# Index score products that may break into projection chains at once, with rope tables, row scales and weight rooms rearranged, in one layer of a hybrid streaming encoder

## The chip, the cores and the metric

The kernel runs on one core of one Trainium2 chip. A core has five engines that work side by side: TensorE (PE) for matrix products, VectorE (DVE), ScalarE (ACT), GpSimd (POOL) and SyncE (SP), which issues the DMAs. The metric is the device time of one execution in microseconds. The kernel before takes 1736.39 us (median of 3 runs, 1735.83 to 1738.16).

## The reference

One layer is run for two request groups that share weights: a prompt of 1024 new positions, and 32 sample positions with 512 cached ones. Width is 1024, heads have 64 channels, there are 8 heads in each mixer.

```python
h = rmsnorm(x);  z = h @ w_in        # q/k/v of mixer A, indexer q, k, weights, q/k/v of mixer B, gates
q_a, k_a = rope(rmsnorm(q_a, g_qn)), rope(rmsnorm(k_a, g_kn));  q_i, k_i = rope(q_i), rope(k_i)
# mixer A: the indexer scores all keys, and each query attends to its top k of them
score = einsum('bqhl,bqh->bql', relu(q_i @ k_i), w_i);  idx = top_k(score, topk)
o_a = softmax(q_a @ k_a[idx]) @ v_a[idx]
# mixer B: stick-breaking attention, strictly causal
o_b = (exp(log_sigmoid(s) - tail(softplus(s)))) @ v_b
h = x + (sigmoid(gate_a) * (o_a @ w_ba) + sigmoid(gate_b) * (o_b @ w_bb)) @ w_out
y = h + relu(rmsnorm(h) @ w_up)**2 @ w_down
```

The outputs are y and the new keys and values of both mixers and of the indexer, for both groups. Everything is float32.

## The kernel before, in words

**Numbers.** Each float32 matrix product is done as three products of a faster format: an operand is split into a high part (a ScalarE copy that rounds) and a low part (the rest, by a subtraction on GpSimd or VectorE), and high x high, high x low and low x high are added. The 1056 positions form nine tiles: eight of 128 rows and one of 32 (`NEW`). A weight unit is 128 x 512: one DMA into `wst`, the high half `wh` from ScalarE, the low half `wl` from GpSimd. `wh` and `wl` have a ring of five rooms each (`WB`).

**The order of the work.** Nothing is issued when it is written in the code. A planner (`Plan`) records every operation with its engine, rank and an estimated cost. When a pool of memory is closed, it plays the five engines forward and issues, on each, the ready operation of the lowest rank and then of the oldest number. The order so found is fixed at build time, and each engine follows it strictly. Ranks are `FAST` 0, `PREP` 1 (weight loads and splits), `MAIN` 2, `FILL` 3 (the long projection chains) and `SLOW` 4. A rule concerns TensorE alone: while it is in a `FILL` chain, another ready product may break in only when it has been ready for longer than its patience:

```python
if eng == PE and self.row is not None and n.row is None and at - n.ready < n.wait:
```

Patience is `WAIT[0]` = 1000 ns for the whole first part, up to the end of mixer A's projection.

**The stages in turn.** (1) The index stage: x is scaled and split, the indexer's queries are projected in two halves (`index_projection`, tiles `s` in three PSUM banks), rotated, and transposed (`rr`); the sums of squares give the row scales `rs` (128 x 9). (2) `spread_rs` makes from `rs` a row `rb` of 1056 scales that is the same on all partitions: nine times `ones` times one column of `rs` (tile `rsb`, on GpSimd), a TensorE transpose into a `t` bank, a ScalarE copy. Every projection's result is multiplied by `rb` on VectorE, and only then is its `pj` bank (two of them) free. `index_keys` scales the indexer's keys `kr`, also on GpSimd. (3) `project_b` for four head pairs: chains of 24 products per part for q, k and v of mixer B (`FILL`), and, recorded between pairs 1 and 2, `index_scores`: 12 score parts times 8 heads, each of two products into an `s` bank (`kih`, `kil`), a relu on ScalarE in place, and a multiply-add on VectorE into `score`. (4) `top_k_begin`: 31 rounds of a binary search, in two groups of tiles, each round counting scores on ScalarE and VectorE (`junk`, `cand`, `small`), at rank `SLOW`. (5) `rope_tables` loads the cosines and sines into the projection pool and multiplies them by the gains of q and k on VectorE (`tabc`, `tabs`). `project_a` for four head pairs: per tile a row block of 24 products, then VectorE multiplies by the tables (`ta`, `tb`), GpSimd adds, ScalarE squares; at the end transposes `qk` into `az`. Each pair needs four weight units plus two for v. (6) `top_k` makes the masks; three gates; then the pools are closed, and attention opens its own in the same room. (7) Attention of the first 512 positions of mixer B and then A, with gate chains as filling; `load_o` reads the outputs back from DRAM and splits them, four tiles (e = 4 to 7, ring `sg` of three rooms) before the branch products of mixer B can end; then branch, output projection and the feed-forward part, with the attention of the second half beside it.

The functions of the diff, with the lines of the profile:

Of the kernel before, what the change touches and what calls it, by code (L numbers as in the profile page):

```python
# [9 lines left out]
F32 = mybir.dt.float32  # L10
F32R = mybir.dt.float32r
BF16 = mybir.dt.bfloat16
I32 = mybir.dt.int32
AF = mybir.ActivationFunctionType
ALU = mybir.AluOpType
# [5 lines left out]
KB = D // 128  # L21
# [3 lines left out]
T = SEQ + DEC  # L25
NT = 9
H = 8
HD = 64
# [12 lines left out]
NEW = 8  # L41
WB = 5
# [3 lines left out]
GATES = (2, 3, 4)  # L46
SUMS = 3
ORDER = (*range(8, 16), 5, 6, 7)
WAIT = (1000, 0, 1500)
TOPK = (("a", [2, 3, 4, 7], (2, 7), 0), ("b", [5, 6, 8], (5, 6), 16))  # L50
EARLY, PACE = 14, 3
LATER = 3
FAST, PREP, MAIN, FILL, SLOW = 0, 1, 2, 3, 4
# [365 lines left out]
class Layer:  # L419
# [18 lines left out]
        self.nc.scalar.copy(h, x)  # L438
        self.nc.gpsimd.tensor_sub(l, x, h.bitcast(F32))

    def unit(self, src):

        nc = self.nc
        key = (src.tensor.name, src.offset)
        if key in self.begun:
            return self.begun.pop(key)
        with nc.rank(PREP):
            st = nc.tile(self.wpool, [128, 512], F32, "wst", bufs=3)
            h = nc.tile(self.wpool, [128, 512], F32R, "wh", bufs=WB)
            l = nc.tile(self.wpool, [128, 512], F32R, "wl", bufs=WB)  # L450
            nc.sync.dma_start(st, src)
            self.split(h, l, st)
        return h, l
# [79 lines left out]
    def run(self):  # L533
        nc, a = self.nc, self.a
# [8 lines left out]
        c = lambda shape, dt, name: nc.tile(self.const, shape, dt, name)  # L543
# [41 lines left out]
        self.index_setup()  # L585
        nc.patience = WAIT[0]
        for sl in ((0,), (1, 2), (3,), (4, 5), (6, 7, 8)):
# [3 lines left out]
            for s in sl:  # L591
                self.index_projection(0, s)
                if s >= LATER:
                    self.row_square(s - LATER)
        self.constants()
        for s in range(NT):
            self.index_projection(1, s)
            if s < LATER:
                self.row_square(NT - LATER + s)
# [9 lines left out]
        mk = nc.open("mask", "right")  # L609
        self.mask = [nc.tile(mk, [128, 128 * (t + 1)], BF16, f"mask{t}") for t in range(8)]  # L610
        self.mask.append(nc.tile(mk, [128, LS], BF16, "mask8"))
        self.top = nc.open("top", "right")
        self.index_scores()
        for p in range(2, 4):
            self.project_b(p)
        with nc.rank(SLOW):
# [3 lines left out]
        self.early(*(a["w_qka"][0, j] for j in range(4)))  # L620
        nc.close(self.pr, self.ik)
        self.pr = nc.open("proja")
        self.rope_tables()
        self.sample(self.pr)
        for p in range(4):
            self.project_a(p)
# [2 lines left out]
        for e in GATES:  # L629
            self.gate(e)  # L630
        self.early(*(a["w_g"][e, j] for e in (8, 9) for j in range(2)))
        nc.close(self.pr, self.top)
        nc.patience = WAIT[1]


# [123 lines left out]
    def spread_rs(self):  # L759

        nc = self.nc
        for sl in GROUPS:
            pt = self.bank("t")
            n = sum(rows(s) for s in sl)
            for i, s in enumerate(sl):
                b = nc.tile(self.ip, [128, 128], F32, "rsb", bufs=2)
                nc.gpsimd.tensor_scalar(b, self.ones, self.rs[:, s:s + 1], None, op0=ALU.mult)
                m = rows(s)
                nc.tensor.transpose(pt[:, i * 128:i * 128 + m], b[:m], self.ident[:m, :m])
            nc.scalar.copy(self.rb[:, 128 * sl[0]:128 * sl[0] + n], pt[:, :n])  # L770


    def index_setup(self):
# [173 lines left out]

    def top_k(self):

        nc, tp, tx, size = self.nc, self.top, self.top, self.size  # L950
        for g in self.groups:
            tf = nc.tile(tp, [128, g.n], I32, "tf" + g.name)
            nc.vector.tensor_scalar(tf, g.thr, 0, None, op0=ALU.bitwise_xor)
            tf = tf.bitcast(F32)
            if g.act:
                low = nc.tile(tp, [128, g.n], F32, "low" + g.name)
                for j, t in enumerate(g.tiles):
                    m, L, k = size(t)
                    if t not in g.act:
                        nc.vector.tensor_copy(low[:m, j:j + 1], tf[:m, j:j + 1])  # L960
                        continue
                    pen = nc.tile(tx, [128, 1024], F32, "pen", tag="pre", bufs=1)
                    nc.vector.tensor_scalar(
                        pen[:m, :L], self.score[t][:m], tf[:m, j:j + 1], BIG, op0=ALU.is_lt, op1=ALU.mult)
                    nc.vector.tensor_tensor_reduce(
                        out=pen[:m, :L], in0=pen[:m, :L], in1=self.score[t][:m], scale=1.0, scalar=BIG,
                        op0=ALU.add, op1=ALU.min, accum_out=low[:m, j:j + 1])
                tf = low
            above = g.count(tf, ALU.is_gt)
            need = nc.tile(tp, [128, g.n], F32, "need" + g.name)  # L970
            for j, t in enumerate(g.tiles):
                m, L, k = size(t)
                nc.vector.tensor_scalar(
                    need[:m, j:j + 1], above[:m, j:j + 1], -1.0, float(k), op0=ALU.mult, op1=ALU.add)
                sc = self.score[t][:m]
                eq = nc.tile(tx, [128, 1024], BF16, "eq", tag="junkv", bufs=1)
                pre = nc.tile(tx, [128, 1024], F32, "pre", bufs=1)
                nc.vector.tensor_scalar(eq[:m, :L], sc, tf[:m, j:j + 1], None, op0=ALU.is_equal)
                nc.vector.tensor_tensor_scan(pre[:m, :L], eq[:m, :L], eq[:m, :L], 0.0, op0=ALU.add, op1=ALU.bypass)
                nc.vector.scalar_tensor_tensor(  # L980
                    pre[:m, :L], pre[:m, :L], need[:m, j:j + 1], eq[:m, :L], op0=ALU.is_le, op1=ALU.mult)
                nc.vector.scalar_tensor_tensor(
                    pre[:m, :L], sc, tf[:m, j:j + 1], pre[:m, :L], op0=ALU.is_gt, op1=ALU.add)
                nc.gpsimd.tensor_scalar(self.mask[t][:m, :L], pre[:m, :L], -NEG, NEG, op0=ALU.mult, op1=ALU.add)
        for j in range(4):
            if j:
                nc.sync.dma_start(self.mask[8][32 * j:32 * j + 32], self.mask[8][0:32])
            nc.sync.dma_start(self.fqs[32 * j:32 * j + 32], self.fq[:DEC, NEW, j::4])


    def rope_tables(self):
        nc, a, pr = self.nc, self.a, self.pr
        self.tc_ = nc.tile(pr, [128, NT, 2, HD], F32, "tabc")
        self.ts_ = nc.tile(pr, [128, NT, 2, HD], F32, "tabs")
        C = nc.tile(pr, [128, NT, HD], F32, "ropec")
        S = nc.tile(pr, [128, NT, HD], F32, "ropes")
        g = nc.tile(pr, [128, 2, HD], F32, "gqk")
        nc.sync.dma_start(C, a["rope_c"])
        nc.sync.dma_start(S, a["rope_s"])
        nc.sync.dma_start(g, a["g_qk"].unsqueeze(0).to_broadcast([128, 2, HD]))  # L1000
        for j in range(2):
            nc.vector.tensor_mul(self.tc_[:, :, j], C, g[:, j].unsqueeze(1).to_broadcast([128, NT, HD]))
            gx = g[:, j].rearrange("p (s e) -> p s e", s=2)[:, ::-1, :].unsqueeze(1).to_broadcast([128, NT, 2, 32])
            nc.vector.tensor_mul(
                self.ts_[:, :, j].rearrange("p t (s e) -> p t s e", s=2),
                S.rearrange("p t (s e) -> p t s e", s=2), gx)

    def project_v(self, p, mixer, w, vout):

# [48 lines left out]

    def project_a(self, p):
        nc, pr, a = self.nc, self.pr, self.a  # L1060
        units = [self.unit(a["w_qka"][p, j]) for j in range(4)]
        qk = nc.tile(pr, [128, NT, 4, HD], F32, "qk", bufs=1)
        ss = nc.tile(pr, [128, NT, 4], F32, "ss", bufs=2)
        nc.gpsimd.memset(qk[:, NEW], 0.0)
# [25 lines left out]
        rsb = self.rs.unsqueeze(2).to_broadcast([128, NT, 4])  # L1090
# [15 lines left out]
        for j, dst in ((0, self.dq), (1, self.dk)):  # L1106
            for sl in GROUPS:
                n = sum(rows(s) for s in sl)
                pt = self.bank("t")
# [234 lines left out]
    def load_o(self, g, j, tag="sg", bufs=3):  # L1344

        nc = self.nc
        for e in range(4 * j, 4 * j + 4):
            if not g.i and e == H // 2 - 1:
                for i, o in enumerate(self.kept):
                    z = slice(64 * i, 64 * i + 64)  # L1350
                    with nc.rank(FAST):
                        nc.scalar.copy(g.h[z, e], o)
                        nc.vector.tensor_sub(g.l[z, e], o, g.h.bitcast(F32)[z, e])
                continue
            with nc.rank(PREP):
                o32 = nc.tile(self.op, [128, g.w], F32, "o32", tag=tag, bufs=bufs)
                nc.sync.dma_start(o32, self.do[2 * e:2 * e + 2, :, g.lo:g.lo + g.w].rearrange("g e t -> (g e) t"))
                self.split(g.h[:, e], g.l[:, e], o32)

# [300 lines left out]
    def ffn_group(self, g, late=iter(())):  # L1660
# [62 lines left out]
        def beside(n):  # L1723
# [3 lines left out]
            while done >= PACE:  # L1727
                done -= PACE
                nc.patience = WAIT[2]
                with nc.behind():  # L1730
                    next(late, None)
                nc.patience = WAIT[1]

# [100 lines left out]
```

## Time and profile before

| | |
|---|---|
| median of 3 runs | 1736.39 us (1735.83 to 1738.16) |
| profiled execution, its own time | 1734.1 us |
| span of its instructions | 1732.3 us |
| PE busy | 1707.9 us (99%) |
| DVE, ACT, POOL busy | 1225.2, 1046.0, 1006.3 us |
| mean granted TensorE clock | 0.999 |

The span runs from the first instruction to the last. An engine is busy while an instruction of its runs, not while it waits. Products overlap in the array, so the time that a product takes up is read from start to start and not from its duration. Every operation is recorded by one helper, so all rows bear its line, L410, and are told apart by the tiles: `rsb<-ones,rs` writes `rsb` and reads `ones` and `rs`. "SPq" is SyncE's queue of DMA issues. In the list of waits a row gives the engine that waited, the tile, who released it, the total, the number and the longest.

### The profile page before, as it was taken

How to read it: one execution, taken by the hardware profiler on the slowest of the kernel's cores; microseconds unless marked ns; L12 is line 12 of the kernel's file. 1: busy time of each engine (PE TensorE's matmuls, PEld its weight loads, DVE VectorE, ACT ScalarE, POOL GpSimd, SP SyncE). 2: the span in 40 equal slices, each digit the busy share in tenths (PEclk: the TensorE clock that was granted, in tenths of full speed). 3: DMA queues.
4: the chain of work that ended last, by engine and by line, in shares of the span. 5: the costliest groups of instructions: out<-in, count | busy, mean ns of one | idle time of the engine just before them, and what ended most of it. 6: DMA issues, size and time to landing. Idle time of an engine off the chain costs nothing.

```text
span 1732.3 us, 32764 instructions
## 1 busy us (share of the span) xinstructions
PE 1707.9 (99%) x11154; PEld 1569.7 (91%) x11154; DVE 1225.2 (71%) x2474; ACT 1046.0 (60%) x2274; POOL 1006.3 (58%) x838
## 2 busy tenths in 40 slices
PE   8999999999999999999999999999999999999999
PEld 7889998999999889988888888888889999999999
DVE  8545578999966645899987777675455674766667
ACT  6544488887245666777765665462524685747473
POOL 5533231334465676799974544586467794646563
PEclk9999999999999999999999999999999999999999
DMA  6344352444665767656277475574675656556565
GB/s 216 117 140 125 106 148 98 137 138 138 181 176 152 189 200 208 191 166 186 88 220 223 142 246 172 183 240 169 237 254 184 181 169 193 170 178 176 177 179 175
DMA packets 190424, 301.78 MB, mean 174 GB/s; under 512 B 31281, under 2 KB 60561, under 8 KB 190257
## 3 DMA queue, kind: packets, MB, share of 16 engines
q1 hardware_dynamic: 189824, 299.35, 56.7%
q8 instruction: 88, 1.44, 0.3%
q14 instruction: 80, 0.65, 0.1%
q10 hardware_dynamic: 432, 0.34, 0.1%
HBM read 211.80 MB, written 87.70 MB: 173 GB/s over the span
## 4 chain that ended last, share of the span: by engine, by line
PE 86%; DVE 5%; DMA 4%; POOL 2%; issue 2%; ACT 2%; SPq 0%; ACTq 0%; DVEq 0%; POOLq 0%
PE pj L410 62%; PE s L410 13%; PE t L410 4%; PE o L410 4%; PE pd L410 3%; DMA o<-do 1%; DVE rem L410 1%; POOL wl L410 1%; DMA k<-dk 1%; DVE xl L410 1%; DVE tt L410 1%; DMA wst<-w_up 0%; DVE junk L410 0%; ACT wh L410 0%; ACT xh L410 0%
## 5 line engine op out<-in xcount | busy, mean ns | idle before, releaser
L410 PE MATMUL pj<-xh,wh 128*128 128x512 f32 (+1 forms) x1808 | 618.6, 343 | 2.4 <-ACT xh L410 1.8
L410 PE MATMUL pj<-xh,wl 128*128 128x272 f32 (+1 forms) x1808 | 617.5, 342 | 0.6 <-POOL wl L410 0.6
L410 PE MATMUL pj<-xl,wh 128*128 128x512 f32 (+1 forms) x1808 | 616.4, 342 | 0.0
L410 POOL TENSOR_TENSOR wl<-wst,wh 128x512 fp32r<-128x512 f32 x243 | 346.1, 1431 | 248.2 <-ACT wh L410 218.2
L410 PEld LDWEIGHTS pj<-xh,wh 128*128 128x128 f32 x1808 | 340.5, 189 | 35.5 <-ACT xh L410 1.9
L410 PEld LDWEIGHTS pj<-xh,wl 128*128 128x128 f32 x1808 | 340.4, 188 | 33.6 <-POOL wl L410 1.3
L410 PEld LDWEIGHTS pj<-xl,wh 128*128 128x128 f32 x1808 | 340.6, 188 | 32.5 <-issue 0.2
L410 ACT CAST wh<-wst 128x512 fp32r<-128x512 f32 x260 | 159.9, 621 | 139.6 <-PE pj L410 93.9
L410 POOL TENSOR_TENSOR wl<-raw,wh 128x512 fp32r<-128x512 f32 x84 | 119.7, 1429 | 98.2 <-ACT wh L410 93.9
L410 DVE TENSOR_TENSOR_SCAN rem<-rem 128x896 f32<-128x896 f32 (+6 forms) x66 | 124.2, 1899 | 22.7 <-ACT rem L410 19.3
L410 ACT CAST wh<-raw 128x512 fp32r<-128x512 f32 x118 | 73.3, 623 | 83.4 <-PE pj L410 50.6
L410 ACT ACTIVATE junk<-score,cand 128x384 bf16<-128x384 f32 (+1 forms) x124 | 115.9, 935 | 8.0 <-DVE cand L410 5.9
L410 POOL TENSOR_TENSOR p<-p,rem 128x895 f32<-128x895 f32 (+6 forms) x66 | 110.3, 1684 | 17.7 <-DVE rem L410 16.7
L410 DVE TENSOR_TENSOR tt<-t,tt 128x512 fp32r<-128x512 f32 (+2 forms) x168 | 100.1, 619 | 27.1 <-ACT tt L410 26.3
L410 ACT CAST tt<-t 128x512 fp32r<-128x512 f32 (+2 forms) x168 | 85.9, 539 | 45.9 <-PE t L410 30.9
L410 PEld LDWEIGHTS o<-tt,v 128*128 128x128 f32 x640 | 93.2, 189 | 12.9 <-DVE tt L410 3.2
L410 PE MATMUL o<-tt,v 128*128 128x256 f32 (+1 forms) x640 | 100.5, 278 | 1.5 <-DVE tt L410 1.1
L410 PE MATMUL pj<-gh,wl 128*128 128x272 f32 x352 | 101.3, 289 | 0.0
L410 PE MATMUL pj<-gl,wh 128*128 128x272 f32 x352 | 101.1, 288 | 0.0
L410 PE MATMUL pj<-gh,wh 128*128 128x272 f32 x352 | 101.1, 289 | 0.0
L410 POOL TENSOR_TENSOR wl<-rb,wh 128x512 fp32r<-128x512 f32 x55 | 77.3, 1406 | 34.3 <-ACT wh L410 30.1
L410 PE MATMUL s<-k,q 128*128 128x384 f32 (+5 forms) x384 | 94.8, 357 | 2.0 <-DMA k<-dk 1.0
(337 smaller groups left out, 4002.6 us busy)
## 6 DMA issues: line engine op xcount, KB each, us to landing
q<-dq SPq DMA_DIRECT2D x64, 256.0 KB, 5.3
k<-dk SPq DMA_DIRECT2D x48, 256.0 KB, 3.8
v<-dv SPq DMA_DIRECT2D x48, 256.0 KB, 4.0
raw<-w_down SPq DMA_DIRECT2D x47, 256.0 KB, 3.4
wst<-w_up SPq DMA_DIRECT2D x43, 256.0 KB, 3.0
wst<-w_g SPq DMA_DIRECT2D x42, 256.0 KB, 3.9
raw<-w_up SPq DMA_DIRECT2D x42, 256.0 KB, 3.1
wst<-w_down SPq DMA_DIRECT2D x39, 256.0 KB, 3.3
```

The source lines that it names most:

```text
L410: fn(*args, **kw)
```

## The change

1. `WAIT` gets a fourth value, 0, which is the patience of the index score products.
2. `spread_rs`: the nine scalings go from GpSimd to ScalarE (odd tiles) and VectorE (even tiles), all at rank `FAST`, as do the copies into `rb`. Eight of them have one wide tile `rsb` in place of two rooms in turn.
3. The first weight unit of `project_b` is begun before the second half of the index projection.
4. `rope_tables` is recorded before the index scores and has a pool of its own. The cosines and sines are loaded straight into both halves of the tables (four loads in place of two, in runs of 64 elements), and six GpSimd products at rank `SLOW` multiply them by the gains in place.
5. The weights of mixer A's pairs 1 and 3 get four rooms each for `wh` and `wl` in the projection pool; pairs 0 and 2 stay in the common ring.
6. `top_k`'s scratch tiles `pre` and `pen` move to a pool of their own.
7. `load_o`: for the first half, the tile e = 7 is loaded into the ring `pb` in place of `sg`.

```diff
-WAIT = (1000, 0, 1500)
+WAIT = (1000, 0, 1500, 0)
...
-    def unit(self, src):
+    def unit(self, src, room=None):
...
+        pool, n = (room, 4) if room else (self.wpool, WB)
         with nc.rank(PREP):
             st = nc.tile(self.wpool, [128, 512], F32, "wst", bufs=3)
-            h = nc.tile(self.wpool, [128, 512], F32R, "wh", bufs=WB)
-            l = nc.tile(self.wpool, [128, 512], F32R, "wl", bufs=WB)
+            h = nc.tile(pool, [128, 512], F32R, "wh", bufs=n)
+            l = nc.tile(pool, [128, 512], F32R, "wl", bufs=n)
...
         self.constants()
+        self.early(a["w_qb"][0, 0])
...
+        rope = nc.open("rope", "right")
+        self.rope_tables(rope)
         self.top = nc.open("top", "right")
+        nc.patience = WAIT[3]
         self.index_scores()
+        nc.patience = WAIT[0]
...
         self.pr = nc.open("proja")
-        self.rope_tables()
+        self.pre = nc.open("pre", "right")
...
+        rsb = nc.tile(self.pr, [128, T], F32, "rsb", tag="vt", bufs=1)
...
-                b = nc.tile(self.ip, [128, 128], F32, "rsb", bufs=2)
-                nc.gpsimd.tensor_scalar(b, self.ones, self.rs[:, s:s + 1], None, op0=ALU.mult)
+                b = rsb[:, 128 * s:128 * s + 128] if s != NEW else nc.tile(self.ip, [128, 128], F32, "rsb", bufs=1)
+                with nc.rank(FAST):
+                    if s % 2:
+                        nc.scalar.activation(b, self.ones, AF.Copy, scale=self.rs[:, s:s + 1])
+                    else:
+                        nc.vector.tensor_scalar(b, self.ones, self.rs[:, s:s + 1], None, op0=ALU.mult)
...
-            nc.scalar.copy(self.rb[:, 128 * sl[0]:128 * sl[0] + n], pt[:, :n])
+            with nc.rank(FAST):
+                nc.scalar.copy(self.rb[:, 128 * sl[0]:128 * sl[0] + n], pt[:, :n])
...
-        C = nc.tile(pr, [128, NT, HD], F32, "ropec")
-        S = nc.tile(pr, [128, NT, HD], F32, "ropes")
...
+        for tab, src in ((self.tc_, a["rope_c"]), (self.ts_, a["rope_s"])):
+            for j in range(2):
+                nc.sync.dma_start(tab[:, :, j], src)
         for j in range(2):
...
+            with nc.rank(SLOW):
+                c = self.tc_[:, :, j]
+                nc.gpsimd.tensor_mul(c, c, g[:, j].unsqueeze(1).to_broadcast([128, NT, HD]))
+                for i in range(2):
+                    z = self.ts_[:, :, j, 32 * i:32 * i + 32]
+                    nc.gpsimd.tensor_mul(z, z, g[:, j, 32 - 32 * i:64 - 32 * i].unsqueeze(1).to_broadcast([128, NT, 32]))
...
-        units = [self.unit(a["w_qka"][p, j]) for j in range(4)]
+        units = [self.unit(a["w_qka"][p, j], pr if p % 2 else None) for j in range(4)]
...
-                o32 = nc.tile(self.op, [128, g.w], F32, "o32", tag=tag, bufs=bufs)
+                if not g.i and e == KB - 1:
+                    o32 = g.tmp("o32", "pb", 3)
+                else:
+                    o32 = nc.tile(self.op, [128, g.w], F32, "o32", tag=tag, bufs=bufs)
```

More of the change, by code (lines that the diff above doesn't have):

```diff
@@ L631, in run @@
         self.early(*(a["w_g"][e, j] for e in (8, 9) for j in range(2)))
-        nc.close(self.pr, self.top)
+        nc.close(self.pr, self.pre, self.top, rope)
         nc.patience = WAIT[1]
@@ L948, in top_k @@
     def top_k(self):
-        nc, tp, tx, size = self.nc, self.top, self.top, self.size
+        nc, tp, tx, size = self.nc, self.top, self.pre, self.size
         for g in self.groups:
@@ L975, in top_k @@
                 sc = self.score[t][:m]
-                eq = nc.tile(tx, [128, 1024], BF16, "eq", tag="junkv", bufs=1)
+                eq = nc.tile(tp, [128, 1024], BF16, "eq", tag="junkv", bufs=1)
                 pre = nc.tile(tx, [128, 1024], F32, "pre", bufs=1)
@@ L988, in top_k, with rope_tables @@
             nc.sync.dma_start(self.fqs[32 * j:32 * j + 32], self.fq[:DEC, NEW, j::4])
[L991 to L994, printed above, removed]
-        C = nc.tile(pr, [128, NT, HD], F32, "ropec")
-        S = nc.tile(pr, [128, NT, HD], F32, "ropes")
-        g = nc.tile(pr, [128, 2, HD], F32, "gqk")
-        nc.sync.dma_start(C, a["rope_c"])
-        nc.sync.dma_start(S, a["rope_s"])
+    def rope_tables(self, pool):
+        nc, a = self.nc, self.a
+        self.tc_ = nc.tile(pool, [128, NT, 2, HD], F32, "tabc")
+        self.ts_ = nc.tile(pool, [128, NT, 2, HD], F32, "tabs")
+        g = nc.tile(pool, [128, 2, HD], F32, "gqk")
         nc.sync.dma_start(g, a["g_qk"].unsqueeze(0).to_broadcast([128, 2, HD]))
+        for tab, src in ((self.tc_, a["rope_c"]), (self.ts_, a["rope_s"])):
+            for j in range(2):
+                nc.sync.dma_start(tab[:, :, j], src)
         for j in range(2):
[L1002 to L1006, printed above, removed]
+            with nc.rank(SLOW):
[4 more added lines that the diff above has]
+                    nc.gpsimd.tensor_mul(z, z, g[:, j, 32 - 32 * i:64 - 32 * i].unsqueeze(1).to_broadcast([128, NT, 32]))
     def project_v(self, p, mixer, w, vout):
```

## The prediction

> **What bounds the kernel now.** I read first the engines' busy time, then the list of who TensorE (PE) waited for, then the busy time by stretch.
>
> ```profile
> PE 1707.9 (99%) x11154; PEld 1569.7 (91%) x11154; DVE 1225.2 (71%) x2474; ACT 1046.0 (60%) x2274; POOL 1006.3 (58%) x838
> ```
> ```profile
> PE s L410 <- ACT ih L410: 5.2, 1, 5.2
> PE t L410 <- POOL rsb L410: 2.4, 5, 0.8
> PE s L410 <- DVE small L410: 2.1, 1, 2.1
> PE pj L410 <- ACT xh L410: 1.8, 1, 1.8
> PE t L410 <- DVE az L410: 1.4, 1, 1.4
> ...
> PE pj L410 <- POOL wl L410: 0.6, 2, 0.3
> ```
> ```profile
> 280.00:360.00 80.00, 76.27 (x590) 73.11 (x589) 74.82 (x258) 71.08 (x157) 28.86 (x36) 1.00 0.41 121
> 440.00:480.00 40.00, 40.00 (x254) 36.13 (x253) 36.83 (x59) 8.61 (x19) 14.91 (x11) 1.00 0.55 168
> ```
>
> PE sets the end: it is idle 1732.3 - 1707.9 = 24.4 us in all, and the change takes no product away. So only what PE loses in idle time, or at a lowered clock, can be won. Four waits that the edits touch stand in the list: 2.4 (the row scales), 2.1 (the first row blocks of mixer A), 1.8 (attention outputs), 1.4 (az). The 5.2 at the very start is not touched. In the stretches (columns: length, PE, weight load, VectorE, ScalarE, GpSimd) PE is idle 3.73 us from 280 to 360, where VectorE (DVE) is busy 74.82 of 80; from 440 to 480 it isn't idle at all. All five engines run an order written at build time, each strictly in turn; a wait therefore holds everything behind it.
>
> **Row scales (spread_rs).** Here PE loses more than the 2.4 us. The products in order of time, then two stretches' clock:
>
> ```profile
> 81.14 0.28 PE L410 MATMUL pj<-xh,wl 128*128 128x272 f32 x1
> ...
> 85.17 0.33 PE L410 MATMUL t<-ident,rsb 128*128 128x128 f32 x1 [0.25 <-POOL rsb L410]
> 85.25 0.37 PE L410 MATMUL pj<-xh,wh 128*128 128x272 f32 x1
> 85.46 0.29 PE L410 MATMUL pj<-xl,wh 128*128 128x272 f32 x1
> 85.58 0.29 PE L410 MATMUL pj<-xh,wl 128*128 128x272 f32 x1
> ```
> ```profile
> 86.00:89.00 3.00, 3.00 (x14) 2.60 (x13) 0.44 (x1) 1.07 (x2) 1.51 (x2) 0.50 0.04 11
> ```
>
> From 81.14 to 85.25 are 4.11 us. In them one product (0.12, the step from 85.46 to 85.58) and the five transposes of the list of waits (0.08 each, 85.17 to 85.25) do work: 0.52. Lost: 3.6. Then the granted clock is 0.50 for 3.0 us, which loses 3.0 x 0.50 = 1.5. Together 5.1 us. The cause is GpSimd (POOL), which does nine scalings of 0.59 among weight splits:
>
> ```profile
> L410 POOL TENSOR_SCALAR rsb<-ones,rs x9: 592/593/597, 76.2 to 85.7; 128x128 f32<-128x128 f32 x9
> ```
> ```profile
> 70.48 0.16 DVE L410 TENSOR_TENSOR rs<-rs,rw 128x9 f32<-128x9 f32 x1
> ```
> ```profile
> 89.11 0.42 ACT L410 CAST zz<-zb 128x272 fp32r<-128x272 f32 x1
> ```
> ```profile
> L410 DVE TENSOR_SCALAR eq<-score,lowa x4: 420/858/1580, 422.5 to 446.2; 128x384 bf16<-128x384 f32 x1, 128x512 bf16<-128x512 f32 x1, 128x640 bf16<-128x640 f32 x1, 128x1024 bf16<-128x1024 f32 x1
> ```
>
> The scales `rs` are ready at 70.64 (70.48 + 0.16). Afterwards ScalarE (ACT) does four of the scalings, VectorE five, at first rank. No row shows such a 128x128 scaling on either. For ACT I bound it by 0.16 (a tiny instruction) and 0.42 (128x272), and take 0.3, nearer the upper one: 4 x 0.3 = 1.2. For VectorE I bound it by 0.16 and by the slowest one-tensor instruction above, 1.58, and take 0.3 again, somewhat under the 0.42 of 128x384: 5 x 0.3 = 1.5, at worst 5 x 1.58 = 7.9. So the first group (two on each engine) is done at 71.3 to 73.8. The part of `rb` that the first multiplication needs then comes after four transposes (4 x 0.08) and one copy of 512 columns, which I estimate at under 1 us from the 0.42 for 272; with the hand-overs I allow 2 us, and PE needs it only when the two chains in hand end at 81.3. Cover remains in every case: I take 5.0 of it as gained, with 2.5 as the lower bound (the transposes may still stand where PE waits a little) and 5.1 as the upper. GpSimd loses 9 x 0.59 = 5.3 us of work, which lets its weight splits come sooner.
>
> The row for `eq` has 1.58 for 640 columns while its fastest is 0.42 for 384, so some of these wait for something. [...]
>
> **Early weights.** `early(w_qb[0,0])` makes the first unit's low half ready before the first chain. Gain at most the 0.6 us that PE waited for wl in two places; I take 0.3. One more 256 KB load goes ahead of the four of the indexer's second half, beside nothing that PE waits for.
>
> **Index products at patience 0.** Now such a product breaks into a chain only after it has waited 1 us.
>
> ```profile
> L410 PE MATMUL s<-kih,qi x96: 282/339/477, 100.6 to 223.7; 128*128 128x384 f32 x24, 128*128 128x512 f32 x24, 128*128 128x320 f32 x16, 128*32 128x272 f32 x16
> ```
> ```profile
> 154.44 0.29 PE L410 MATMUL s<-kil,qi 128*32 128x272 f32 x1
> 154.57 0.40 PE L410 MATMUL pj<-xl,wh 128*128 128x512 f32 x1
> 154.62 1.35 DVE L410 SCALAR_TENSOR_TENSOR score<-s,wi,score 32x272 f32<-32x272 f32 x3 [1.72 <-ACT s L410]
> 157.31 0.31 PE L410 MATMUL s<-kih,qi 128*128 128x320 f32 x1
> ```
> ```profile
> 150.00:175.00 25.00, 25.00 (x153) 22.57 (x153) 14.34 (x30) 10.71 (x27) 6.35 (x7) 1.00 0.47 151
> 250.00:275.00 25.00, 25.00 (x162) 22.92 (x161) 20.29 (x69) 23.08 (x51) 5.19 (x4) 1.00 0.36 120
> ```
>
> 96 score chunks come in threes, one for each bank: 123.1 / 32 = 3.85 us a round. VectorE has read the last bank at 154.62 + 1.35 = 155.97, the next product starts at 157.31: 1.3 us of waiting. So the scores end up to 32 x 1.3 = 43 us sooner, I take 25. To PE this is worth nothing by itself, since PE is full (25.00 of 25.00) both while scores and while the counts of the top-k that follow run beside the chains. Breaking a chain more often costs nothing that a row shows: from the last index product to the chain's next are 0.13 us, the pace of 272 columns. At 0.01 us of resolution and some 64 more breaks, two changes each, the upper bound is 1.3 us; I take 0.
>
> **Rope tables.** Before, their loads wait for the room of the projection pool, and four VectorE products stand ahead of the first reads of the banks.
>
> ```profile
> 291.64 0.74 DVE L410 TENSOR_TENSOR tabc<-ropec,gqk 128x576 f32<-128x576 f32 x1
> ...
> 294.31 0.41 DVE L410 TENSOR_TENSOR ta<-s,tabc 128x256 f32<-128x256 f32 x1
> ```
> ```profile
> 292.85 0.29 PE L410 MATMUL pj<-xh,wl 128*128 128x272 f32 x1
> 295.20 0.36 PE L410 MATMUL s<-wh,xh 128*128 128x256 f32 x1 [2.06 <-DVE small L410]
> ```
>
> PE starts nothing for 2.35 us, less the one product 2.2. The products go to GpSimd, at last rank, beside the index stage, where it is busy 6.35 of 25. Two are of 576 columns, four of 288; by the 1.43 us of a 512-column GpSimd subtraction (below) that is 2 x 1.6 + 4 x 0.8 = 6.4 us, in 18.65 idle ones. Five loads (four tables, the gains) go through SP's queue there instead of three at 283. If a product stood ahead of a weight split and its load were late, the split would be late; the cover is a whole chain. I take -2.2, bounds -2.7 (the four products, which leave a full VectorE) and 0 (counts fill the place, and the wait comes back at the next row block).
>
> **The az wait, and top-k moved forward.** 25 us fewer of counts lie in 280 to 440. All that PE could win there beyond the 2.2 is 3.73 - 2.2 = 1.5 us. I take a third, -0.5; bounds -1.5 and +1.
>
> ```profile
> L410 DVE TENSOR_SCALAR cand<-small x62: 140/160/164, 228.2 to 408.5; 128x4 int32<-128x4 int32 x31, 128x3 int32<-128x3 int32 x31
> ```
> ```profile
> 485.60 0.95 POOL L410 MEMSET qz<- 128x1024 f32 x1
> ```
>
> The end of top-k frees the room in which attention begins (485.60). That may come 15 to 25 us sooner; PE is full there with gates, so again 0.
>
> **Rooms for mixer A's weights.** Splits move, their number stays; PE's waits for wl are 0.6 in all. 0.
>
> **The last attention output** (load_o, e = 7).
>
> ```profile
> 631.35 2.53 POOL L410 TENSOR_TENSOR xl<-o,xh 128x512 fp32r<-128x512 f32 x2 [0.72 <-ACT xh L410]
> ```
> ```profile
> 632.75 0.54 SPq L410 DMA_DIRECT2D o<-do  x1
> ```
>
> Three rooms serve four loads: the fourth is issued at 632.75, when the first is split, and PE waits for it the 1.8 us of the list. In another ring it can be issued with the others. -1.8; at worst 0, if the next wait is for w_bb.
>
> **New waits.** Apart from the named ones and the start, PE's idle time is 24.4 - 2.4 - 2.1 - 1.8 - 1.4 - 5.2 - 0.6, about 11 us, scattered. The whole order after 80 us is written anew, so these fall anew: +2, bounds -4 and +9.
>
> **Sum:** -5.0 - 0.3 - 2.2 - 0.5 - 1.8 + 2.0 = -7.8 us. The profiled execution took 1734.1 (span 1732.3, 1.8 around it), so 1726.3; the median of the runs is 2.3 above it, 1736.39. Forecast: 1728.6. A measurement can tell about 0.2%, 3.5 us, from no change, so under 1732.9 is faster, over 1739.9 slower.
>
> **Rivals.**
> (1) *Better.* The shift of top-k also empties the rest of 280 to 360 (1.5 rather than 0.5) and new waits come out at their lower bound: -5.1 - 0.3 - 2.7 - 1.5 - 1.8 - 4 = -15.4, 1721. For it: VectorE is the only engine that is full there. Against: it stays nearly full.
> (2) *A wait takes the place of the removed.* VectorE, busy 74.82 of 80, fills the tables' place with counts (0 instead of 2.2), az stays, the output's wait turns into one for weights (0), and spread_rs keeps half (2.5). With new waits at +2: -0.8, 1735.6, no change. For it: each of these waits is the last of several in a strict order. Against: at 81 us nothing else is due.
> (3) *Slower: GpSimd between attention and the gates.* With attention 15 to 25 us sooner, its products come between the splits of the gates' 11 x 2 = 22 weight units.
>
> ```profile
> L410 POOL TENSOR_TENSOR wl<-wst,wh 128x512 fp32r<-128x512 f32 x243 | 346.1, 1431 | 248.2 <-ACT wh L410 218.2
> L410 POOL TENSOR_TENSOR p<-p,rem 128x895 f32<-128x895 f32 (+6 forms) x66 | 110.3, 1684 | 17.7 <-DVE rem L410 16.7
> ```
>
> Each split behind one such product is 1.68 later. If the lead of the splits is used up for 9 of 22, PE loses 15 us, net +7.3: 1743.7. It decides from 7 on (7 x 1.68 = 11.8, net +4). Against: only 0.6 us of such waits now, and splits rank ahead of attention.
> (4) *The patience does not bind,* because the banks come free late: then scores end at 224 as before. That changes only terms that I put at 0 or 0.5, and stays in the forecast.
>
> **How the numbers follow.** Forecast 0.58 (its own range 1724 to 1733), rival 1: 0.10, rival 2: 0.19, rival 3: 0.13. Faster 0.68, same 0.19, slower 0.13. The range reaches from rival 1 to the near end of rival 3, 1720 to 1739.
>
> **What would show it.** Right: no wait of PE for rsb and no stretch near 81 us at half clock; rb's copies before 78; index products over by 200; no tabc on VectorE and no wait of 2 us at the first row blocks; cand ends before 390; the fourth o load issued with the other three. Wrong: PE's idle time still above 20 us, waits for wl of more than 3 us, or a second stretch at half clock.

## The result, and the profile after

The changed kernel takes 1724.03 us (median of 5 runs, 1723.17 to 1729.22) against 1735.83 (5 runs, 1734.88 to 1738.16): a ratio of 0.9936, 95% interval 0.992 to 0.9953, or 11.8 us less. The forecast of 1728.6 and its range held. The profiled execution happened to be the slowest of the five, 1729.22, with a span of 1727.4. So the two profiles differ by 4.9 us of span (1732.3 to 1727.4), not by 11.8, and can account for no more than that.

Engines' busy time and PE's list of waits after the change:

```profile
PE 1705.2 (99%) x11154; PEld 1570.7 (91%) x11154; DVE 1216.1 (70%) x2475; ACT 1052.3 (61%) x2282; POOL 1002.4 (58%) x835
```
```profile
PE s L410 <- ACT ih L410: 4.8, 2, 4.4
PE o L410 <- DVE tt L410: 1.9, 2, 1.3
PE t L410 <- POOL rr L410: 1.8, 2, 1.4
PE s L410 <- ACT xh L410: 1.3, 1, 1.3
PE o L410 <- ACT tt L410: 1.2, 1, 1.2
PE o L410 <- POOL vcs L410: 1.2, 1, 1.2
PE t L410 <- issue: 1.0, 1, 1.0
```

All four waits that the edits aim at are gone: rsb (2.4), the first row blocks (2.1), ACT xh at 637 us (1.8) and az (1.4). Yet PE's idle time is still 1727.4 - 1705.2 = 22.2 us, after 24.4: others stand in their places.

PE's busy time fell too, by 1707.9 - 1705.2 = 2.7 us, for the same 11154 products, although this execution lost more to the clock than the one before: 3.4 us after and 1.8 before, both worked out below. At full clock the products thus took some 1706.1 before and 1701.8 after, 4.3 us less. Two other profiles, both at a mean clock of 1.000, differ in the same way. The first has the patience alone, the second the whole change but for the rope tables (both below):

```profile
PE 1705.5 (99%) x11154; PEld 1569.3 (91%) x11154; DVE 1216.3 (70%) x2474; ACT 1049.3 (61%) x2276; POOL 1002.4 (58%) x838
```
```profile
PE 1701.6 (99%) x11154; PEld 1568.6 (91%) x11154; DVE 1218.7 (71%) x2479; ACT 1053.0 (61%) x2282; POOL 1000.7 (58%) x829
```

The ends of products are modelled in the profile, so some of this may be idle time that it counts as busy. Among which products it lies was not found.

By three stretches, first of the kernel before, then of the changed one (columns: length, PE, weight load, VectorE, ScalarE, GpSimd, granted clock, DMA):

```profile
70.00:100.00 30.00, 27.29 (x157) 23.31 (x156) 9.99 (x22) 10.27 (x22) 24.47 (x31) 0.94 0.42 116
100.00:440.00 340.00, 336.27 (x2316) 313.91 (x2316) 264.66 (x782) 240.22 (x591) 114.88 (x125) 1.00 0.43 129
440.00:1130.00 690.00, 683.85 (x4082) 603.86 (x4081) 508.55 (x873) 423.82 (x876) 456.97 (x336) 1.00 0.62 183
```
```profile
70.00:100.00 30.00, 27.07 (x163) 23.08 (x162) 15.79 (x48) 13.21 (x32) 18.87 (x25) 1.00 0.45 117
100.00:440.00 340.00, 339.13 (x2340) 316.69 (x2339) 285.35 (x783) 241.82 (x587) 131.10 (x130) 1.00 0.44 133
440.00:1130.00 690.00, 684.32 (x4078) 607.37 (x4077) 478.65 (x848) 432.74 (x891) 447.87 (x335) 1.00 0.62 184
```

PE's idle time goes from 2.71 to 2.93 us around the row scales, from 3.73 to 0.87 up to the end of mixer A's projection, and from 6.15 to 5.68 in attention and the feed-forward part. The first stretch gains by its clock (0.94 to 1.00: 0.06 x 30 = 1.8 us), not by less waiting. Why it waits as long as before shows in VectorE's and GpSimd's order of the changed kernel, and in PE's:

```profile
71.27 4.40 DVE L410 TENSOR_SCALAR rsb<-ones,rs 128x128 f32<-128x128 f32 x5
...
75.69 0.43 DVE L410 TENSOR_TENSOR qi<-t,qi 64x256 fp32r<-64x256 f32 x1
```
```profile
71.60 3.80 POOL L410 TENSOR_TENSOR wl<-wst,wh 128x512 fp32r<-128x512 f32 x3
```
```profile
77.04 0.39 PE L410 MATMUL pj<-xh,wl 128*128 128x512 f32 x1
78.84 0.31 PE L410 MATMUL t<-ident,rr 32*128 32x32 f32 x2 [1.41 <-POOL rr L410]
```
```profile
L410 DVE TENSOR_SCALAR rsb<-ones,rs x5: 277/1321/1334, 71.3 to 75.4; 128x128 f32<-128x128 f32 x5
L410 ACT ACTIVATE rsb<-ones,rs x4: 387/388/397, 71.5 to 72.4; 128x128 f32<-128x128 f32 x4
```

The fastest of VectorE's scalings takes 0.28 us, one 0.45, three 1.32, beside three GpSimd splits of 3.80 / 3 = 1.27 each; ScalarE's take 0.39. The kernel before already had this: there two small products (`wi`, 128x72) stood beside the same splits and took 1.24 and 1.21 us, while after the change, with the splits over, the two take 0.50 together. First the kernel before, then the changed one:

```profile
71.56 1.24 DVE L410 TENSOR_TENSOR wi<-wi,rs 128x72 f32<-128x72 f32 x1
```
```profile
75.49 0.73 POOL L410 TENSOR_TENSOR rr<-ta,tb 32x256 f32<-32x256 f32 x1 [0.29 <-DVE tb L410]
```
```profile
78.08 0.71 POOL L410 TENSOR_TENSOR rr<-ta,tb 32x256 f32<-32x256 f32 x1 [2.68 <-DVE tb L410]
```

So VectorE reaches the sources of the last `rr` 2.6 us later (GpSimd starts it at 78.08, not 75.49), and PE waits 1.41 for it.

The last index product starts at 188.4 (223.7 before), and attention's first instruction comes at 476.2 (485.60 before):

```profile
L410 PE MATMUL s<-kih,qi x96: 283/339/442, 95.2 to 188.4; 128*128 128x384 f32 x24, 128*128 128x512 f32 x24, 128*128 128x320 f32 x16, 128*32 128x272 f32 x16
```
```profile
L410 POOL MEMSET qz<- x1: 952/952/952, 476.2 to 476.2; 128x1024 f32 x1
```

One thing that no edit touches also differs: the clock. In the five executions the mean granted clock was 1.000 four times and 0.998 in the profiled one; over the 85 executions of the kernel before that stand beside the experiments it was 0.9975. A mean clock of 0.0025 below 1 costs 0.0025 x 1733 = 4.3 us on average, against 0.7 after: an estimate of some 3.6 of the 11.8 us. What the profiled one lost, and where:

```profile
669.40:672.00 2.60, 1.38 (x12) 1.19 (x10) 0.29 (x1) 2.23 (x4) 1.86 (x3) 1.00 1.00 223
672.00:676.00 4.00, 4.00 (x19) 3.89 (x19) 1.83 (x4) 2.33 (x5) 0.48 (x1) 0.51 0.71 223
676.00:680.00 4.00, 4.00 (x24) 4.00 (x24) 0.44 (x1) 0.62 (x1) 1.91 (x2) 0.64 0.33 99
```

One wait of 1.22 us (POOL vcs) lies in the first row; the clock is at half for most of the 8 us behind it, which costs 4 x 0.49 + 4 x 0.36 = 3.4 us, nearly three times the wait.

### The profile page after: what moved, and what is told of

Read it like the earlier page. It is cut to its first block, busy times and chain, and to the rows that moved or that the text cites. A ratio compares the mean times of both kernels' runs of the same rounds, so it can differ in the third digit from the quotient of the medians.

```text
span 1727.4 us, 32804 instructions
## 1 busy us (share of the span) xinstructions
PE 1705.2 (99%) x11154; PEld 1570.7 (91%) x11154; DVE 1216.1 (70%) x2475; ACT 1052.3 (61%) x2282; POOL 1002.4 (58%) x835
## 4 chain that ended last, share of the span: by engine, by line
PE 87%; DVE 6%; DMA 2%; issue 2%; POOL 1%; ACT 1%; SPq 0%; ACTq 0%; DVEq 0%; POOLq 0%
PE pj L410 63%; PE s L410 12%; PE t L410 5%; PE o L410 4%; PE pd L410 3%; DVE xl L410 1%; DVE rem L410 1%; DVE junk L410 1%; POOL wl L410 1%; DMA x<-xT 0%; DMA raw<-w_down 0%; DMA q<-dq 0%; DVE tb L410 0%; DVE tt L410 0%; DMA vc<-cva 0%
## 5 line engine op out<-in xcount | busy, mean ns | idle before, releaser
L410 PE MATMUL pj<-xl,wh 128*128 128x272 f32 (+1 forms) x1808 | 618.4, 343 | 0.9 <-DVE xl L410 0.9
L410 PE MATMUL pj<-xh,wh 128*128 128x272 f32 (+1 forms) x1808 | 617.7, 342 | 0.5 <-DVE vt L410 0.3
L410 POOL TENSOR_TENSOR p<-p,rem 128x895 f32<-128x895 f32 (+6 forms) x66 | 105.6, 1612 | 28.2 <-DVE rem L410 25.6
L410 DVE TENSOR_TENSOR_SCAN rem<-rem 128x896 f32<-128x896 f32 (+6 forms) x66 | 114.0, 1747 | 11.1 <-ACT rem L410 10.8
```

Source lines behind the costliest of these rows:

```text
L410: fn(*args, **kw)
```

## The experiments

Ratios are to the kernel before, run on the same chip beside it, with 95% intervals. The changed kernel was not run again beside them, so a difference to it is one of two ratios, and its own (0.992 to 0.9953) is uncertain by some 3 us either way.

**One part alone.** Each is the kernel before with one part of the diff. The new `spread_rs`:

```diff
-                nc.gpsimd.tensor_scalar(b, self.ones, self.rs[:, s:s + 1], None, op0=ALU.mult)
+                with nc.rank(FAST):
+                    if s % 2: nc.scalar.activation(b, self.ones, AF.Copy, scale=self.rs[:, s:s + 1])
+                    else: nc.vector.tensor_scalar(b, self.ones, self.rs[:, s:s + 1], None, op0=ALU.mult)
```

> The kernel before with the new spread_rs alone (scalings on ScalarE and VectorE at first rank). Theory A (the parts are worth what their own stalls cost): the wait for rsb and the half clock at 86 us go, 3 to 5 us less than before, 0.997 to 0.998. [...] Rival C (the gain of the change comes from moving top-k forward): no difference clear of noise here.

Measured: 0.9988 (0.9979 to 0.9996), 2.1 us less. VectorE's scalings take 1.32 us in the median here too. The wait for rsb and the half clock at 86 us are gone, as theory A said, but the gain stays below its 3 to 5 us; PE's longest wait from 70 to 100 is now one of 0.8 us for rr. The stretch from 70 to 100:

```profile
70.00:100.00 30.00, 28.53 (x186) 25.27 (x184) 14.88 (x38) 12.31 (x30) 20.82 (x27) 1.00 0.43 120
```

Idle time falls from 2.71 to 1.47 us and the clock stays up (1.8), so 3 us are gained here; not all of it arrives at the end. The mean clock of its eleven executions is 0.9973, no higher than that of the kernel before beside it (0.9973): the drop that was avoided here does not show in it, as the clock drops elsewhere (in this profile to 0.84 from 30 to 40 us and to 0.66 from 640 to 650).

The patience alone:

```diff
+        nc.patience = 0
         self.index_scores()
+        nc.patience = WAIT[0]
```

> The kernel before with patience 0 for the index score products alone. Theory A: scores end some 25 to 30 us sooner, top-k's counts too, and the time stays within 1.5 us of before (0.999 to 1.001), because PE is full while both run. Rival C: at least 3 us of the whole gain are here (0.998 or less), through a VectorE that is free at the end of mixer A's projection.

Measured: 0.9989 (0.998 to 0.9999), 1.9 us less, with the scores over at 195. That lies at the edge of theory A and below what rival C asks.

The rope tables alone:

```diff
+        rope = nc.open("rope", "right")
+        self.rope_tables(rope)     # loads into the tables, products on GpSimd
         self.top = nc.open("top", "right")
...
-        self.rope_tables()
+        self.pre = nc.open("pre", "right")
```

> The kernel before with the rope tables alone made early on GpSimd (with the scratch pool of top-k that makes room for them). Theory A: the wait of 2.1 us at the first row blocks of mixer A goes, 1.5 to 2.5 us less (0.9985 to 0.999). Rival: VectorE is nearly full there, counts take the place of the tables, and the time stays as before (0.9995 to 1.0005).

Measured: 0.9993 (0.9982 to 1.0005). The wait of 2.1 us is gone from the list, the time not clear of no change; both readings stay possible.

The ring of the last attention output alone:

```diff
-                o32 = nc.tile(self.op, [128, g.w], F32, "o32", tag=tag, bufs=bufs)
+                o32 = g.tmp("o32", "pb", 3) if not g.i and e == KB - 1 else nc.tile(self.op, [128, g.w], F32, "o32", tag=tag, bufs=bufs)
```

> The kernel before with the last attention output in the ring pb alone. Theory A: PE's wait of 1.8 us for ACT xh at 637 us goes, 1 to 2 us less (0.999). Rival: another wait stands right behind it (weights of the branch, or cached values), time as before; a wait short enough may also decide whether the clock drops there, then up to 3 us.

Measured: 1.0009 (1.0 to 1.0017), the rival. ACT xh is gone from the list, and this stands in its place:

```profile
PE s L410 <- DMA k<-dk: 3.2, 3, 1.6
PE t L410 <- POOL p L410: 2.4, 2, 1.7
```

The four add up to -0.0021 (0.9988, 0.9989, 0.9993, 1.0009), 3.6 us. The whole gave 0.0064. The rooms for mixer A's weights were never tried by themselves, and the early first unit only together with the row scales, below.

**One part undone.** Each is the changed kernel with one part taken back. Patience 1000 again:

```diff
-WAIT = (1000, 0, 1500, 0)
+WAIT = (1000, 0, 1500, 1000)
```

> The changed kernel with patience 1000 ns for the index score products again. Theory A (parts add up; alone the patience gave 2.6 us): 2 to 3 us slower than the changed kernel, 0.995 to 0.9955 of before. Theory C (the patience frees VectorE at the end of mixer A's projection, and the other parts are worth more next to it): at least 4 us slower than the changed kernel, 0.996 or more. Theory D (what counts is how often the clock drops): its executions have a mean clock of 0.999 or less where the changed kernel has 1.000.

Measured: 1.0012 (1.0003 to 1.0022), 1738.3 us: by the ratios (1.0012 - 0.9936) 13 us slower than the changed kernel, and slower than the kernel before. Its mean clock is 0.9991, which just misses theory D's 0.999 and explains about 1 us of that. Up to 440 us it waits little more than the changed kernel (340 - 338.42 = 1.58 us); the rest is later, in its stretches:

```profile
100.00:440.00 340.00, 338.42 (x2335) 315.54 (x2334) 256.87 (x759) 239.44 (x591) 119.71 (x127) 1.00 0.46 133
440.00:1130.00 690.00, 676.46 (x4037) 597.64 (x4036) 490.90 (x869) 419.65 (x868) 439.80 (x330) 1.00 0.61 180
```

13.54 us of idle time in attention and the feed-forward part, where no index product runs. So the size is theory C's and the place is not: C looked for it at the end of mixer A's projection.

The rope tables late on VectorE again (the old function, called where it was, with the rest of the change):

```diff
-        rope = nc.open("rope", "right")
-        self.rope_tables(rope)
...
+        self.rope_tables()
```

> The changed kernel with the rope tables made late on VectorE again. Theory A: 1 to 2.5 us slower than the changed kernel, 0.9945 to 0.995 of before, and the wait of 2 us of the first row blocks is back. Rival (with the counts of top-k 40 us sooner, VectorE has room for the tables): as fast as the changed kernel, 0.9935.

Measured: 0.993 (0.9917 to 0.9943), 1723.72 us, as fast as the changed kernel. But not for the rival's reason. The waits that the tables cause are back, and a quieter later part pays for them:

```profile
100.00:440.00 340.00, 337.68 (x2332) 315.44 (x2331) 286.73 (x783) 242.37 (x588) 122.45 (x123) 1.00 0.43 130
440.00:1130.00 690.00, 687.25 (x4107) 610.47 (x4106) 484.04 (x855) 435.62 (x894) 459.41 (x339) 1.00 0.62 186
```

2.32 us idle instead of 0.87 up to 440, and 2.75 instead of 5.68 after it.

The ring of three rooms again:

```diff
-                if not g.i and e == KB - 1: o32 = g.tmp("o32", "pb", 3)
```

> The changed kernel with the last attention output in the ring of three rooms again. Theory A: the wait for ACT xh of about 1.8 us is back, 1 to 2 us slower than the changed kernel (0.9945 of before). Rival (alone it gave nothing, 1.0009): no difference, 0.9935, or a little faster.

Measured: 0.9967 (0.9955 to 0.9979), 1730.75 us: 5 us slower than the changed kernel by the ratios, more than any theory said, and from a part that alone gave nothing. Theory A's wait for ACT xh is not back either; from 440 us on, these two lead its list:

```profile
PE t L410 <- POOL p L410: 2.7, 2, 2.1
PE s L410 <- DMA k<-dk: 2.5, 3, 2.0
```

The row scales on GpSimd again, and no early first unit (both together):

```diff
-        self.early(a["w_qb"][0, 0])
...
+                nc.gpsimd.tensor_scalar(b, self.ones, self.rs[:, s:s + 1], None, op0=ALU.mult)
```

> The changed kernel with the row scales on GpSimd again and without the early first weight unit of mixer B. Theory A: 3 to 5 us slower than the changed kernel (0.996 of before), with waits for rsb of 2.4 us and a drop of the clock at 86 us. Theory B (alone it gave 2.2 us): 2 to 3 us slower, 0.995. Theory D: the mean clock of its executions is lower by at least 0.0005 (1 us or more), since the idle time at 81 us makes the clock drop in most executions.

Measured: 0.9997 (0.9986 to 1.0008), 1736.46 us: 11 us more than the changed kernel by the ratios. The wait for rsb is back (2.3 us), and the mean clock is 0.9973, lower by 0.0023 than in the changed kernel, 4 us: D holds for that share. In its profile a wait of 3.0 us (DVE xl) at 724 us is also new.

Undone, the parts are worth 13, 0, 5 and 11 us by their ratios; together far more than the 11.8 there are. No sum of parts explains that. So the last runs show what a new order alone does.

**No part changed, only the order.** In both kernels, one number of the planner's estimate:

```diff
-CHANGE = 20
+CHANGE = 30
```

> The kernel before, with one number of the planner's own estimate changed (30 in place of 20 ns for a change between a chain and other products): no work is added, taken away or given another rank, but the order of most instructions after the first stage is found anew. Theory A (the gain is that of the stalls that the parts remove): within 2 us of before, 0.999 to 1.001. Theory E (a new order is a new draw of the waits after 440 us, worth several us either way): anywhere from 0.996 to 1.004, with 3 us or more of difference more likely than not.

Measured: 1.0022 (1.0011 to 1.0034), 1738.7 us, 3.8 us slower: theory A's 2 us do not hold, theory E's 3 us or more do.

> The changed kernel, with the same number changed. Theory A: within 2 us of the changed kernel, 0.9925 to 0.9950 of before. Theory E: as far from the changed kernel as the kernels with one part undone, up to 14 us slower; the local gains (no wait for rsb, 100 to 440 us at less than 1.5 us of idle time) stay, the waits after 440 us are another draw: 0.994 to 1.000.

Measured: 1.0012 (1.0003 to 1.0021), 1738.48 us: 13 us slower than the changed kernel by the ratios, with every part of the change in it. The index products end at 185, the clock's mean is 0.9979. Its longest waits from 100 to 440, and its stretches:

```profile
PE t L410 <- DVE vs L410: 2.2, 1, 2.2
PE t L410 <- DVE az L410: 0.8, 1, 0.8
```
```profile
100.00:440.00 340.00, 336.38 (x2318) 314.14 (x2317) 285.85 (x780) 240.43 (x578) 128.51 (x129) 0.99 0.43 129
440.00:1130.00 690.00, 680.12 (x4048) 602.13 (x4048) 472.01 (x846) 423.70 (x882) 433.41 (x329) 0.99 0.61 181
```

Theory A is refuted. Theory E holds in size (up to 14 us slower) but not in all it said: the ratio lies just beyond its 1.000, and even the gain before 440 us is not safe (3.62 us idle instead of 0.87), because a wait for VectorE's `vs` has come up in mixer A's projection. Beside the kernel before in its own new order (1.0022), this one is 0.0010 faster, 1.7 us, and the two intervals overlap. Both kernels became slower with 30; whether each order is a draw or 30 is simply the worse estimate, one other value can't tell.

**Mending what the trace shows.** All nine scalings on ScalarE, to see whether rr then comes sooner:

```diff
-                    if s % 2:
-                        nc.scalar.activation(b, self.ones, AF.Copy, scale=self.rs[:, s:s + 1])
-                    else:
-                        nc.vector.tensor_scalar(b, self.ones, self.rs[:, s:s + 1], None, op0=ALU.mult)
+                    nc.scalar.activation(b, self.ones, AF.Copy, scale=self.rs[:, s:s + 1])
```

> The changed kernel with all nine scalings of the row scales on ScalarE. [...]

Measured: 0.9993 (0.9984 to 1.0002), 1734.94 us, 10 us slower than the changed kernel by the ratios. The nine take 0.387 us each, and the wait for rr is gone, but not because rr is ready sooner: GpSimd starts the last rr at 78.04, no sooner than in the changed kernel (78.08), and in the new order PE comes to it only at 80.59 (78.84 in the changed kernel). Idle time from 70 to 100 falls only from 2.93 to 2.07, since a wait for kr grows, and the clock drops there (0.94). What took the scalings' place on VectorE, next to the same splits, is the first row below; behind it VectorE waits for ScalarE, which now does nine scalings (VectorE in order of time):

```profile
71.88 2.50 DVE L410 TENSOR_TENSOR wi<-wi,rs 128x72 f32<-128x72 f32 x2
75.73 0.42 DVE L410 TENSOR_TENSOR qi<-t,qi 64x256 fp32r<-64x256 f32 x1 [1.35 <-ACT qi L410]
```

The two products are back at 1.25 us each, as in the kernel before.

With the scalings of the indexer's keys on ScalarE too:

```diff
-                nc.gpsimd.tensor_scalar(
-                    kr[:m, i], self.ka[:m, s].unsqueeze(1).to_broadcast([m, 2, HD]), self.rs[:m, s:s + 1], None, op0=ALU.mult)
+                nc.scalar.activation(
+                    kr[:m, i], self.ka[:m, s].unsqueeze(1).to_broadcast([m, 2, HD]), AF.Copy, scale=self.rs[:m, s:s + 1])
```

> As the run with all scalings of the row scales on ScalarE, and the nine scalings of the indexer's keys (kr) there too instead of on GpSimd. Theory: the waits for kr of 1.0 and 0.5 us at 86 to 91 us go as well, 2.5 to 3.5 us less lost between 70 and 100 us than in the changed kernel. The whole time then goes by the new draw after 440 us: 0.990 to 0.997 of before.

Measured: 0.9931 (0.9919 to 0.9943), 1723.66 us, not distinguishable from the changed kernel. Locally it falls short: 0.5 us less idle time (30 - 27.62 = 2.38) instead of 2.5 to 3.5, because one wait of 1.9 us for kr stays, now on ScalarE.

## Why the prediction was right or wrong

The direction and the range were right, the size was short: -7.8 said, -11.8 measured. The working behind it was right for most of the edits and wrong in what it took to decide the total.

Most of its own signs came true: no wait for rsb, no half clock near 81 us, the index products over by 200, no tabc on VectorE, cand at its end by 365.9. But the first copy of rb came at 79.8, not before 78. And two signs of being wrong came true as well in the profiled execution: PE's idle time of 22.2 us, above 20, and a second stretch at half clock, at 672 to 680 us.

So the nearness of 1728.6 to 1724.03 is in part luck. Without the 1.5 for the clock, the sum held about 6.3 us less idle time, and the two profiles show 2.2. What made up for it stood in no term: products that took 4.3 us less at full clock, where the working had said that only idle time and a lowered clock can be won, and executions with hardly a drop of the clock.

*Row scales (-5.0).* Mis-sized. The wait for rsb and the half clock at 86 us went, as said. The step that failed is the price of VectorE's scalings, 0.3 us: three of five took 1.32. The rows of `wi` in the profile before, 1.24 us for 72 columns beside the same splits, already showed such a price. The 1.32 was inside the bound of 1.58, but its consequence was looked for in the wrong place. The working asked only whether rb would be late (it wasn't: its copy came at 79.8, before the 81.3 at which the working needed it) and not what stands behind the scalings on VectorE: the sources of rr, for which PE waited 1.41. That the scalings hold up rr is read from VectorE's rows, which are busy almost without a gap from 71.27 to 77.9; the run with all scalings on ScalarE does not confirm it, since rr comes as late there, now behind ScalarE. Of 5.0, the clock's 1.8 less 0.2 of idle time remained here; alone, the part gave 2.1. The rows of rsb, 1.32 beside splits of 1.27, speak against scalings on VectorE next to GpSimd's splits; "Cover remains in every case" was true of rb alone.

*Early weights (-0.3).* PE's wait for wl, 0.6 before, is no longer in the list.

*Patience (0).* The mechanism was right. Scores ended 35 us sooner (25 taken, 43 the bound); alone it gave 1.9 us, a little more than the 0 put down. Rival 4, that the patience does not bind, is refuted. Undone, it cost 13 us, but after 440 us, where no index product runs.

*Rope tables and az (-2.7 together).* Right, in this order. The stretch of the changed kernel that had 3.73 us of idle time before:

```profile
280.00:360.00 80.00, 79.40 (x618) 76.40 (x617) 74.25 (x257) 71.28 (x159) 27.84 (x32) 1.00 0.39 116
```

0.60 us are left, 3.1 less. That it can be had is shown; that it is kept is not, as the redrawn order had 3.62 us from 100 to 440.

*Top-k moved forward.* Attention began 9 us sooner, not 15 to 25. The three gates of mixer A's stage still came ahead of it.

*The last attention output (-1.8).* The wait went, though that the last load is issued with the other three does not show: SyncE's queue has loads of o at 618.3 and 629.4 us where the kernel before had them at 632.75 and 635.14, and the trace doesn't tell which tile each is. The changed kernel's high halves of that stage begin within 6 us now, the last at 633.3:

```profile
L410 ACT CAST xh<-o x5: 605/621/634, 627.4 to 633.3; 128x512 fp32r<-128x512 f32 x5
```

Alone, the part was worth nothing; waits for k and for GpSimd's p stood in its place.

*New waits (+2, bounds -4 and +9).* Between the two profiles this term is small: from 440 to 1130 us, PE's idle time is 6.15 before and 5.68 after. Between orders that hold the change, or most of it, it is large, and it was treated as a remainder: the three at 1724 us have 2.75 (tables late), 5.24 (kr on ScalarE too) and 5.68, the one at 1731 has 7.55, and the four at 1735 to 1738 have 8.42 to 13.54. The bounds were about right, the weight was not: the redrawn orders (1.0022 and 1.0012) show that the planner's order moves either kernel by more than any part does alone. Of the 11 us that the working called scattered, 3.8 also lie behind PE's last product (its end at 1728.5 of 1732.3), where nothing can fall anew.

*The clock.* The working priced one drop at one place. The executions show that drops come and go: 0.995 to 0.999 for the same kernel before, 1.000 in four of five after. Of the 3.6 us from this, the sum had counted 1.5 under the row scales; the other 2.1 are about half of the 4.0 that it lacked.

*Rivals.* Rival 2's mechanism, a wait in the place of the removed, is what rr shows after, and k and p where the ring was changed alone, though not with its total. Rival 3, the slower case, did not happen by its mechanism: no wait for wl in the list. Yet two orders that hold most or all of the change are slower than before, by other waits (k, vs, p, pb).

What is shown, then: the edits remove the waits they aim at, locally worth some 4 to 5 us (1.8 - 0.2 + 2.86 from the stretches from 70 to 440). What is not shown is that the change as such makes this kernel 11.8 us faster; the same change in another order made it 0.0012 slower. The four orders that hold the whole change or add to it stand at 0.9936, 1.0012, 0.9993 and 0.9931, the two orders of the kernel before at 1 and 1.0022. PE's idle time from 440 to 1130 us goes with it; which feature of the order sets that, and makes 1723 or 1738 us of it, was not found.

## What to carry to other kernels

Where a planner orders the instructions, time an edit against a second order of the same kernel, with one number of the plan nudged; until the gain stands out from that, the edit's share and the draw's can't be told apart. When an instruction is moved to another engine, ask what stands behind it there, and how long it takes beside the work of the engine it was taken from (here 1.32 us beside GpSimd's splits of 1.27, and 0.28 behind them). A wait of PE can cost more than its length (one of 1.22 us was followed by half clock that lost 3.4), so executions should be compared with their clocks beside them.

## What the runs showed of the hardware

A wait of 1.22 us was followed by half clock for most of 8 us (3.4 us lost), one of 2.06 us in the kernel before (295 us) by none: the granted clock there was 1.00 from 291 to 306. So the longer wait was not the one with the drop. Ahead of the drop PE was busy 1.38 of 2.60 us, from 669.40 to 672.00, and after its start no wait in that profile's list is longer than 1.4 us. What sets off the drop was not shown.

Two kinds of VectorE instructions beside GpSimd's splits took about the splits' time (1.27 us) and not their own: 1.32 us for a scaling of 128 columns (0.28 behind the splits), 1.25 for a product of 72 columns (0.23 with no split beside it).
